# Block inverse of a delta-rule scan: subtractions on GpSimd, products on VectorE

## The chip, the cores and the metric

The kernel runs on one core of one Trainium2 chip. The engines are TensorE (PE in the profile, with PEld for its weight loads), VectorE (DVE), ScalarE (ACT), GpSimd (POOL) and SyncE (SP), which issues most of the DMAs. Every engine works through its own queue of instructions in order and waits at semaphores for the others. The metric is the device time of one execution in microseconds (us).

## The reference

One layer of a backbone over 128 prompt tokens and 2048 sample tokens: a modulated RMSNorm, one wide input projection, three mixers side by side, a gated merge and an output projection. The mixer that matters here is a gated delta rule, computed in chunks; each chunk solves a unit lower triangular system:

```python
m = eye + bc[..., :, None] * jnp.einsum('bnhik,bnhjk->bnhij', kc, kc) * dec_strict
rhs = jnp.concatenate([vc * bc[..., None], kc * (bc * jnp.exp(gam))[..., None]], axis=-1)
sol = lax.linalg.triangular_solve(m, rhs, left_side=True, lower=True, unit_diagonal=True)
...
def step(s, inp):
    u0_, w_, qk_, qg_, kd_, gl_ = inp
    u = u0_ - jnp.einsum('bhck,bhkv->bhcv', w_, s)
    o = jnp.einsum('bhck,bhkv->bhcv', qg_, s) + jnp.einsum('bhij,bhjv->bhiv', qk_, u)
    s = gl_[..., None, None] * s + jnp.einsum('bhck,bhcv->bhkv', kd_, u)
```

The other two mixers are a spatial gate over chunks of 128 tokens (whose norms are called `vss` and whose products `st` below) and a Fourier transform over grid and channels (tiles `xc`, `Y`, `X`, `yT`).

## The kernel before

All GEMMs are written as three float16 products (high by high, high by low, low by high), 512 token columns at a time. They fill TensorE's queue through the whole kernel. The delta mixer runs beside them as a Python generator, `delta()`, that is advanced a step at a time by a pacer: each stretch of GEMM work that is written down lets the generator write down some more of its own instructions. The tile framework then orders each engine's instructions by priority and by its own estimate of when each can run, so a change of engine moves neighbours too.

`delta()` goes through 17 blocks of 128 tokens, in five groups (the prompt block alone, then four groups of four). For each block `prep` normalises keys and queries (row sums on ScalarE, then `ss`, a power of -0.5 on GpSimd), turns tiles on TensorE (`tok`, `T`), forms the triangular matrices (`n`) and stores them (`nd`, `kv` and others, through GpSimd's DMA queue among others). While `prep` works on one group, `base_inverse` inverts the diagonal blocks of the group before: 32 by 32 unit triangular blocks, two directions, one block on each partition. Tile X (in `XB`, first half) holds the blocks, `tmp` (second half of `XB`) the products, E the growing inverse.

The inverse is 31 rounds, from k = 31 down to 1. Round k multiplies k entries of one column of X with 32 - k entries of row k of E, and subtracts these k x (32 - k) products from the rows of E above it. So round k needs E as round k + 1 left it, and `tmp` is written anew in each round. After the rounds four pairs of instructions on ScalarE and VectorE split E into high and low float16 halves, written over `XB`, and DMAs store them (`ei`).

The inverse of the last group, `base_inverse(4)`, is written after all of `prep`. Behind it the pool that holds `XB` and E is closed and another is opened in its place. That one holds the tiles of the scan: `R`, `T`, `Q`, `N`, `ES`, which GpSimd sets to zero, before SyncE loads `ES` and GpSimd copies parts of it into `T` and `R`. The scan's first matmul (`b<-ES,N`) follows. The scan itself needs the inverses in order of the groups.

Around the last inverse the Fourier mixer runs: TensorE makes `X` from PSUM through ScalarE and VectorE, GpSimd copies a mirrored half (`X<-X`), and when a group of channels is done GpSimd forms the gated products `st<-sg,yT` and stores them (`br<-st`).

Four engines are called through a thin recording object, `_InTurn`. It can force the instructions written in certain places to keep their order. Because every call goes through one line of it, nearly all instructions of before bear the line L180 in the profile; tiles tell them apart.

Of the kernel before, what the change touches and what calls it, by code (L numbers as in the profile page):

```python
# [15 lines left out]
ALU = mybir.AluOpType  # L16
# [152 lines left out]
class _InTurn:  # L169


    def __init__(self, tc, engine):
        self.tc, self.engine, self.kept, self.last, self.newest = tc, engine, False, None, None

    def __getattr__(self, name):
        f = getattr(self.engine, name)

        def call(*args, **kw):
            with self.tc.issue_after(self.last.ins) if self.kept and self.last is not None else ExitStack():
                self.newest = f(*args, **kw)  # L180
            if self.kept:
                self.last = self.newest
            return self.newest

        return call

    def queued(self):

        return self.tc.issue_after(self.newest.ins)


@with_exitstack
def hybrid_flow_kernel(ctx: ExitStack, tc: tile.TileContext, x_prompt, x_sample, state_delta, c, c_ctx, w_ada,
# [4 lines left out]
    G, V, A, PE = [_InTurn(tc, e_) for e_ in (nc.gpsimd, nc.vector, nc.scalar, nc.tensor)]  # L198
# [9 lines left out]
    def sb(pl, shape, tag, dt=F32, bufs=None):  # L208
        kw = {} if bufs is None else {"bufs": bufs}
        return pl.tile(list(shape), dt, tag=tag, name=nm(tag), **kw)  # L210
# [31 lines left out]
    newest, gated_, queued = [None], [None], [False]  # L242
# [847 lines left out]
    def base_inverse(g):  # L1090
        nt = len(GROUPS[g])
        nb = 16 * nt
        XB = sb(dq, [P, 2048], "XB")
        X, tmp = XB[:, 0:1024], XB[:, 1024:2048]
        E = sb(dq, [P, 1024], "E")
        if nt < 4:
            V.memset(X, 0.0)
            V.memset(tmp, 0.0)
        b3 = lambda t_: t_.rearrange("p (j i) -> p j i", j=32)
        for d in range(2):  # L1100
            SY.dma_start((X if d == 0 else tmp)[64 * d:64 * d + nb, :], ndD[g][d].rearrange("t h (b j) i -> (t h b) (j i)", b=4))
        for _ in range(8):
            yield 0
        with V.queued():
            V.tensor_copy(b3(X[64:P, :]), tmp[64:P, :].rearrange("p (i j) -> p j i", j=32))
        G.memset(E, 0.0)
        G.memset(E[:, 0:1024:33], 1.0)
        X3, E3 = b3(X), b3(E)
        for k in range(31, 0, -1):
            n_ = 32 - k  # L1110
            t3 = tmp[:, 0:k * n_].rearrange("p (j i) -> p j i", j=k)
            V.tensor_tensor(t3, X3[:, 0:k, k:k + 1].to_broadcast([P, k, n_]), E3[:, k:k + 1, k:32].to_broadcast([P, k, n_]), ALU.mult)
            V.tensor_tensor(E3[:, 0:k, k:32], E3[:, 0:k, k:32], t3, ALU.subtract)
            if k % 2 == 0:
                yield 1
        both = XB.bitcast(F16).rearrange("p (j l w c) -> p j l w c", j=32, l=2, w=2)
        for j0 in (0, 16):
            js = slice(j0, j0 + 16)
            for w, src in ((0, E3), (1, E.rearrange("p (i j) -> p j i", j=32))):
                A.activation(both[:, js, 0, w, :], src[:, js], AF.Copy, scale=FS)  # L1120
                V.scalar_tensor_tensor(both[:, js, 1, w, :], src[:, js], FS, both[:, js, 0, w, :], ALU.mult, ALU.subtract)
                yield 1
            out = [(eD[g][d][js].rearrange("j t (y x) -> (t y) j x", x=128),
                    both[64 * d:64 * d + nb, js].rearrange("p j l w c -> p j (l w c)")) for d in range(2)]
            if g < 4:
                extra.extend(out)
            else:
                SY.dma_start(*out[0])
                A.dma_start(*out[1])
# [277 lines left out]
    def delta():  # L1407
# [5 lines left out]
        for i_, (g, ci, t) in enumerate(seq):  # L1413
            if ci == 0 and g:
                for r_ in base:
                    if r_:
                        yield 1
                base = base_inverse(g - 1)
            for n_, _ in enumerate(prep(g, ci, t, seq[i_ + 1][2] if i_ < 16 else None, held)):
                yield 1  # L1420
                if next(base, 0):
                    yield 1
# [6 lines left out]
        for _ in base_inverse(4):  # L1429
            yield 1  # L1430
# [750 lines left out]
```

## Time and profile before

| what | us |
|---|---|
| three runs | 2149.31, 2153.33, 2158.91 (median 2153.33) |
| the profiled execution, its own time | 2152.75 |
| its span | 2150.9 |
| TensorE busy | 2080.9 |
| VectorE busy | 1363.5 |
| ScalarE busy | 1061.5 |
| GpSimd busy | 751.8 |

The span is what the profiler saw of the profiled execution; 1.85 us lie around it. The mean granted TensorE clock was 0.994. Busy times are sums over the span; the inverses lie between 480 and 876 us, and the scan begins at about 893 us. A row of an engine's timeline reads: start, duration, engine, line, operation, what is written from what, sizes, count, and in brackets the idle time before it and what ended that. The end of a matmul is modelled, so matmuls that follow each other overlap in the rows; their spacing is the start of one to the start of the next.

### The profile page before, as it was taken

What the parts mean: (1) busy time and instruction counts of PE and PEld (TensorE: products, weight loads), DVE (VectorE), ACT (ScalarE), POOL (GpSimd) and SP (SyncE); (2) the same over time, 40 slices, a digit from 0 to 9 for tenths busy, and PEclk for the clock granted to TensorE, in tenths of its full rate; (3) what the DMA queues carried; (4) which work ended last, traced back from release to release, by engine and by line L of the source; (5) the groups of instructions that cost most, each with busy time, mean ns of one, the idle gap of its engine ahead of it and who ended that gap; (6) DMA issues with size and microseconds to landing.
All of it is one profiled execution on the core that took longest, in us unless ns stands there. A gap on an engine that the chain in (4) does not pass through costs nothing.

```text
span 2150.9 us, 42623 instructions
## 1 busy us (share of the span) xinstructions
PE 2080.9 (97%) x16133; PEld 1194.8 (56%) x16133; DVE 1363.5 (63%) x3100; ACT 1061.5 (49%) x2457; POOL 751.8 (35%) x934
## 2 busy tenths in 40 slices
PE   7999999999999999889899999999999999999997
PEld 4454444455555677777555556555655444444443
DVE  6656854389878798566655555766665554666245
ACT  5554744476555664445544445755554353443112
POOL 0321332223333422442322233345443234343464
PEclk9999999999999999999999999999999999999999
DMA  9525732277876743444645555866664645456862
GB/s 353 219 77 191 264 113 92 72 227 224 255 218 223 239 153 98 124 128 136 222 161 167 169 160 188 254 217 207 208 200 137 210 169 175 167 196 234 342 220 89
DMA packets 222910, 403.25 MB, mean 187 GB/s; under 512 B 39720, under 2 KB 109632, under 8 KB 219888
## 3 DMA queue, kind: packets, MB, share of 16 engines
q1 hardware_dynamic: 167664, 290.84, 42.1%
q0 software_dynamic: 15216, 65.89, 8.1%
q10 hardware_dynamic: 39824, 43.79, 6.1%
q8 instruction: 127, 2.08, 0.4%
q14 instruction: 79, 0.65, 0.1%
HBM read 258.19 MB, written 142.24 MB: 186 GB/s over the span
## 4 chain that ended last, share of the span: by engine, by line
PE 70%; DVE 14%; DMA 6%; issue 4%; ACT 3%; POOL 2%; SPq 1%; ACTq 0%; DVEq 0%; POOLq 0%
PE b L180 70%; DVE n L180 2%; DVE XB L180 2%; DVE E L180 1%; DVE sg L180 1%; DMA st<-br 1%; DMA tw<-tw 1%; DMA ab<-in_w_adb_dram 1%; DVE big L180 1%; DVE S L180 1%; DMA ES<-ei 1%; ACT xh L180 0%; DVE X L180 0%; DVE xl L180 0%; DVE xh L180 0%
## 5 line engine op out<-in xcount | busy, mean ns | idle before, releaser
L180 PE MATMUL b<-xh,whi 128*128 128x512 f16 (+1 forms) x1920 | 651.1, 348 | 3.5 <-DVE sg L180 3.5
L180 PE MATMUL b<-xl,whi 128*128 128x512 f16 (+1 forms) x1920 | 651.6, 348 | 0.0
L180 PE MATMUL b<-xh,wlo 128*128 128x512 f16 (+1 forms) x1920 | 650.4, 348 | 0.0
L180 PEld LDWEIGHTS <-whi 128*128 128x128 f16 x3888 | 355.4, 98 | 324.3 <-issue 9.1
L180 PEld LDWEIGHTS <-wlo 128*128 128x128 f16 x1944 | 190.6, 98 | 175.6 <-issue 2.0
L180 PE MATMUL b<-big,bhi 128*128 128x512 f16 (+1 forms) x960 | 251.5, 347 | 2.3 <-ACT big L180 2.0
L180 ACT ACTIVATE sg<-b,winv 128x512 f32<-128x512 f32 (+1 forms) x180 | 110.8, 618 | 160.5 <-PE b L180 155.2
L180 PE MATMUL b<-big,blo 128*128 128x512 f16 (+1 forms) x480 | 163.0, 347 | 0.0
L180 POOL TENSOR_TENSOR mrow<-mrow,sg 128x512 f32<-128x512 f32 (+1 forms) x80 | 92.9, 1163 | 146.4 <-DVE sg L180 113.3
L180 PEld LDWEIGHTS <-xh 128*128 128x128 f16 x1496 | 117.1, 98 | 30.9 <-issue 3.8
L180 POOL TENSOR_TENSOR cy<-cy,raw 128x545 f32<-128x545 f32 (+1 forms) x48 | 65.8, 1396 | 184.3 <-ACT raw L180 184.3
L180 PEld LDWEIGHTS <-bhi 128*128 128x128 f16 x960 | 86.9, 98 | 75.1 <-issue 1.2
L180 PEld LDWEIGHTS <-xl 128*128 128x128 f16 x1068 | 98.1, 98 | 44.9 <-DMA tw<-tw 1.8
L180 PE MATMUL b<-whi,xh 128*128 128x128 f16 x544 | 92.8, 219 | 1.4 <-DVE sg L180 1.4
L180 PE MATMUL b<-whi,xl 128*128 128x128 f16 x544 | 92.8, 219 | 0.0
L180 PE MATMUL b<-wlo,xh 128*128 128x128 f16 x544 | 92.8, 219 | 0.0
L180 DVE SCALAR_TENSOR_TENSOR wlo<-wst,wsc,whi 128x1024 f16<-128x1024 f32 x52 | 68.1, 1311 | 35.0 <-ACT whi L180 34.9
L180 POOL COPY T<-ES 32x256 f16<-32x256 f16 x68 | 29.6, 436 | 159.7 <-DMA ES<-ei 148.3
L180 ACT ACTIVATE whi<-wst,wsc 128x1024 f16<-128x1024 f32 x52 | 59.4, 1143 | 47.8 <-DVE wsc L180 45.1
L180 POOL TENSOR_TENSOR skn<-skn,ed 128x512 f32<-128x512 f32 x34 | 38.0, 1118 | 124.5 <-DMA skn<-kv 119.9
L180 ACT ACTIVATE wlo<-wst 128x1024 f16<-128x1024 f32 x52 | 55.0, 1058 | 47.5 <-DMA wst<-in_w_blk_dram 44.7
L180 DVE SCALAR_TENSOR_TENSOR sg<-b,binv,sg 128x512 f32<-128x512 f32 (+1 forms) x80 | 53.3, 667 | 39.6 <-PE b L180 38.0
(460 smaller groups left out, 4244.4 us busy)
## 6 DMA issues: line engine op xcount, KB each, us to landing
wst<-in_w_blk_dram SPq DMA_DIRECT2D x58, 512.0 KB, 4.5
pa<-pa POOLq DMA_DIRECT2D x16, 896.0 KB, 4.5
qkv<-cy POOLq DMA_DIRECT2D x12, 1089.0 KB, 5.3
st<-br SPq DMA_DIRECT2D x48, 256.0 KB, 3.2
mrow<-mrg SPq DMA_DIRECT2D x16, 576.0 KB, 4.1
pa<-pa SPq DMA_DIRECT2D x5, 1792.0 KB, 11.1
dc<-dec SPq DMA_DIRECT2D x17, 512.0 KB, 6.0
kq<-qkv SPq DMA_DIRECT2D x34, 256.0 KB, 5.0
```

What stands on the lines that cost most here:

```text
L180: self.newest = f(*args, **kw)
```

## The change

In each round of the block inverse the subtraction is issued on GpSimd (`G`); the product stays on VectorE (`V`). All 31 rounds of all five inverses are affected: 155 instructions go from one queue to the other. The recording object is rewritten too: it passes calls through untouched where no order is kept, and looks up the newest instruction of its engine when asked, in place of remembering it. With the subtraction left on VectorE this second part gives the same order on all five engines; it changes the line numbers that the instructions bear.

```diff
     def __getattr__(self, name):
         f = getattr(self.engine, name)
+        if not self.kept:
+            return f
...
     def queued(self):
-        return self.tc.issue_after(self.newest.ins)
+        e = self.engine.engine
+        newest = next((i for i in reversed(self.tc.nc.cur_bb.bb.instructions) if i.engine == e), None)
+        return ExitStack() if newest is None else self.tc.issue_after(newest)
...
             V.tensor_tensor(t3, X3[:, 0:k, k:k + 1].to_broadcast([P, k, n_]), E3[:, k:k + 1, k:32].to_broadcast([P, k, n_]), ALU.mult)
-            V.tensor_tensor(E3[:, 0:k, k:32], E3[:, 0:k, k:32], t3, ALU.subtract)
+            G.tensor_tensor(E3[:, 0:k, k:32], E3[:, 0:k, k:32], t3, ALU.subtract)
```

The orders of all engines are the same up to the first inverse and again from some way into the scan. Between them three places show what moved. The first is GpSimd's queue at the start of the second inverse, while `prep` works on the third group. Before:

```order
L180 DMA nd_3923<-nd_5836 128x4x32
L180 DMA kv_3818<-tok_5924 128x1024
L180 TENSOR_TENSOR ss_752_5925<-ss_752_5925,mhalf_91 128x4
L180 TENSOR_SCALAR rq_1282<-ss_752_5925 128x4
L180 TENSOR_TENSOR st_6072<-sg_6069,vrow_5622 128x512
L180 DMA br_3916<-st_6072 128x512
```

After:

```order
L1074 DMA nd_3923<-nd_5836 128x4x32
L1045 DMA kv_3818<-tok_5924 128x1024
L1115 TENSOR_TENSOR E_5753<-E_5753,XB_5752 128x31
L1465 TENSOR_TENSOR st_6072<-sg_6069,vrow_5622 128x512
L1115 TENSOR_TENSOR E_5753<-E_5753,XB_5752 128x30x2
L1024 TENSOR_TENSOR ss_752_5925<-ss_752_5925,mhalf_91 128x4
L1467 DMA br_3916<-st_6072 128x512
L1115 TENSOR_TENSOR E_5753<-E_5753,XB_5752 128x29x3
L1038 TENSOR_SCALAR rq_1282<-ss_752_5925 128x4
L1115 TENSOR_TENSOR E_5753<-E_5753,XB_5752 128x28x4
```

A norm (`ss`), a gate product (`st`) and a store now stand between subtractions, and each is behind one that waits for VectorE.

The second place is GpSimd's queue at the end of the last inverse and the start of the scan. Before:

```order
L180 COPY X_1092_8298<-X_1092_8298 128x4x63 x2
L180 TENSOR_TENSOR st_10527<-sg_10172,yT_9570 128x512
L180 TENSOR_TENSOR st_10531<-sg_10231,yT_9570 128x512
L180 TENSOR_TENSOR st_10535<-sg_10329,yT_9570 128x512
L180 DMA br_3917<-st_10527 128x512
L180 MEMSET R_1272_10504 128x1024
```

After:

```order
L1115 TENSOR_TENSOR E_9690<-E_9690,XB_9689 128x4x28
L1465 TENSOR_TENSOR st_10527<-sg_10172,yT_9570 128x512
L1465 TENSOR_TENSOR st_10531<-sg_10231,yT_9570 128x512
L1465 TENSOR_TENSOR st_10535<-sg_10329,yT_9570 128x512
L1115 TENSOR_TENSOR E_9690<-E_9690,XB_9689 128x3x29
L1467 DMA br_3917<-st_10527 128x512
L1467 DMA br_3917<-st_10531 128x512
L1467 DMA br_3917<-st_10535 128x512
L1115 TENSOR_TENSOR E_9690<-E_9690,XB_9689 128x2x30
L1465 TENSOR_TENSOR st_10567<-sg_10564,yT_9570 128x512
L1465 TENSOR_TENSOR st_10599<-sg_10596,yT_9570 128x128
L1115 TENSOR_TENSOR E_9690<-E_9690,XB_9689 128x31
```

Five gate products and three stores stand inside the last three rounds; before, the products came after the inverse and three of them ahead of the scan's memsets.

The third place is TensorE's queue at the scan's first matmul (the one that reads `ES`). Before:

```order
L180 MATMUL b_10854<-wlo_9675,xh_94 128x128
L180 LDWEIGHTS xl_95
L180 MATMUL b_10854<-whi_9674,xl_95 128x128
L180 LDWEIGHTS N_1275_10510
L180 MATMUL b_10784<-ES_10512,N_1275_10510 128x32
```

After:

```order
L250 MATMUL b_11224<-xl_95,whi_10061 128x512
L250 LDWEIGHTS wlo_10062
L250 MATMUL b_11224<-xh_94,wlo_10062 128x512
L250 LDWEIGHTS N_1275_10510
L250 MATMUL b_10784<-ES_10512,N_1275_10510 128x32
```

It stands 24 matmuls of 512 columns and 192 of 128 columns later than before, in another unit of the Fourier mixer. These matmuls are then missing in the stretch that follows: up to the first use of the scan's state (`b<-S,sk`) there are 180 matmuls of 128 columns fewer than before.

More of the change, by code (lines that the diff above doesn't have):

```diff
@@ L172, in __init__ @@
     def __init__(self, tc, engine):
-        self.tc, self.engine, self.kept, self.last, self.newest = tc, engine, False, None, None
+        self.tc, self.engine, self.kept, self.last = tc, engine, False, None
     def __getattr__(self, name):
         f = getattr(self.engine, name)
+        if not self.kept:
+            return f
         def call(*args, **kw):
[L179 to L183, printed above, removed]
+            with self.tc.issue_after(self.last.ins) if self.last is not None else ExitStack():
+                self.last = f(*args, **kw)
+            return self.last
         return call
     def queued(self):
-        return self.tc.issue_after(self.newest.ins)
+        e = self.engine.engine
+        newest = next((i for i in reversed(self.tc.nc.cur_bb.bb.instructions) if i.engine == e), None)
+        return ExitStack() if newest is None else self.tc.issue_after(newest)
 @with_exitstack
```

## The prediction

> **What bounds the kernel now.** I read the page's first lines, then what TensorE waited for between 470 and 900 us (the stretch that holds the five block inverses), then the busy time of each engine in the stretches of the inverses, and last the instructions themselves.
>
> ```profile
> span 2150.9 us, 42623 instructions
> PE 2080.9 (97%) x16133; PEld 1194.8 (56%) x16133; DVE 1363.5 (63%) x3100; ACT 1061.5 (49%) x2457; POOL 751.8 (35%) x934
> ```
>
> TensorE (PE) has work in 97% of the span, and only 70 us are idle. What a change on VectorE (DVE) or GpSimd (POOL) can win is a part of these 70 us; what it can lose has no such limit.
>
> ```profile
> 480.00:557.00 77.00, 76.85 (x546) 45.15 (x545) 71.67 (x202) 43.93 (x136) 24.93 (x32) 1.00 0.79 244
> 557.00:640.00 83.00, 78.58 (x508) 44.55 (x507) 71.59 (x169) 49.93 (x150) 31.53 (x39) 0.98 0.71 223
> 640.00:740.00 100.00, 98.47 (x599) 53.32 (x598) 79.12 (x190) 58.82 (x180) 41.46 (x50) 1.00 0.73 230
> 740.00:822.00 82.00, 79.91 (x1091) 67.72 (x1090) 75.17 (x202) 54.14 (x158) 28.38 (x40) 1.00 0.51 167
> 822.00:892.00 70.00, 62.93 (x822) 49.74 (x819) 48.92 (x130) 28.60 (x59) 21.68 (x31) 1.00 0.40 108
> ```
>
> After the length of the stretch the columns are the busy time of PE, weight loads, DVE, ACT and POOL. The first four rows hold one inverse each, the fifth the last inverse. VectorE is busy 86 to 93% in three of the first four, GpSimd about a third; yet PE is idle for 8.2 us in these four and for 7.1 us in the fifth.
>
> ```profile
> PE b L180 <- DVE sg L180: 3.7, 4, 1.5
> PE b L180 <- POOL T L180: 2.4, 1, 2.4
> PE b L180 <- DVE xc L180: 2.0, 3, 1.4
> PE b L180 <- ACT yT L180: 1.6, 1, 1.6
> PE b L180 <- DVE T L180: 1.2, 3, 0.8
> PE b L180 <- DVE X L180: 1.1, 3, 0.5
> ```
>
> These are the six longest of PE's named waits there (total, times, longest). Those on VectorE sum to 8.0 us: this is nearly all that a relieved VectorE can give back.
>
> **The change, part by part.** *Removed from VectorE: 155 subtractions.*
>
> ```profile
> L180 DVE TENSOR_TENSOR E<-E,XB x155: 190/365/1273, 486.9 to 870.0; 128x31 f32<-128x31 f32 x10, 128x60 f32<-128x60 f32 x10, 128x87 f32<-128x87 f32 x10, 128x112 f32<-128x112 f32 x10
> L180 DVE SCALAR_TENSOR_TENSOR XB<-E,XB x20: 679/862/1067, 556.3 to 873.5; 128x512 f16<-128x512 f32 x20
> 830.00:876.00 46.00, 24.68 (x66) 3.15 (x4) 0.00 (x0) 1.00 0.17 43
> sum 385.00, DVE 126.17 ACT 13.99 POOL 3.29; mean DVE 25.23 ACT 2.80 POOL 0.66
> ```
>
> The last two rows are for tile E alone. Of 126.2 us, 20 splits at a mean of 0.87 us are 17; half of the remaining 109 us are the subtractions: 55 us, 11 us per inverse. Of the last inverse's 24.7 us the four splits take 3.4, and half the rest, 10.7 us, is its 31 products.
>
> *Added to GpSimd: the same 155.*
>
> ```profile
> L180 POOL TENSOR_TENSOR st<-sg,yT 128x512 f32<-128x512 f32 x16 | 20.0, 1270 | 21.9 <-DVE wscb L180 10.3 <-DVE E L180 5.0 <-DVE yT L180 3.9
> L180 POOL TENSOR_TENSOR st<-sg,yT 128x128 f32<-128x128 f32 x4 | 1.8, 456 | 1.4 <-DMA br<-st 1.3
> L180 POOL TENSOR_TENSOR ss<-ss,mhalf 128x4 f32<-128x4 f32 x34 | 36.8, 1084 | 46.4 <-DVE ss L180 41.9 <-DVE vss L180 3.8 <-DVE bss L180 0.2
> L180 POOL DMA_DIRECT2D br<-st x40 | 23.4, 586 | 4.1 <-POOL st L180 3.3 <-POOL E L180 0.4 <-DMA kT<-T 0.3
> L180 POOL COPY X<-X 128x252 f16<-128x252 f16 x32 | 15.1, 480 | 58.9 <-ACT X L180 43.5 <-DVE X L180 15.1
> br<-st POOLq DMA_DIRECT2D x32, 256.0 KB, 2.9
> ```
>
> From 128 elements (456 ns) to 512 (1270 ns) an f32 operation of two inputs grows by 2.12 ns an element, over a fixed 185 ns. Round k has k(32-k) elements, 5456 in 31 rounds: 31 x 0.185 + 5456 x 0.00212 = 17.3 us per inverse, 87 us in all, against 55 us taken off VectorE.
>
> *Added: two hand-overs a round.* The product must now be seen by GpSimd and the difference by VectorE.
>
> ```profile
> 876.54 1.04 DVE L180 TENSOR_TENSOR yT<-b,us 128x256 f32<-128x256 f32 x2
> 877.67 3.73 POOL L180 TENSOR_TENSOR st<-sg,yT 128x512 f32<-128x512 f32 x3 [10.34 <-DVE wscb L180]
> 2124.45 1.07 POOL L180 TENSOR_TENSOR hss<-hss,mhalf 128x1 f32<-128x1 f32 x1
> 2125.55 1.28 DVE L180 SCALAR_TENSOR_TENSOR xh<-xh,hss,fg 128x1024 f32<-128x1024 f32 x1 [0.44 <-POOL hss L180]
> ```
>
> VectorE ends at 877.58 and GpSimd starts at 877.67 (0.09 us); GpSimd ends at 2125.52 and VectorE starts at 2125.55 (0.03). 31 x 0.12 = 3.7 us an inverse. The bare chain of one inverse is then 10.7 + 17.3 + 3.7 = 31.7 us.
>
> *First four inverses.* Each has 82 us or so and its result is wanted only later, so a chain of 32 us plus what it queues behind fits; the PE order hardly moves there. What counts is the queue: the order puts norms (1.08 us each), DMA issues and gate products between the subtractions on GpSimd, each now behind a subtraction that waits for a product. PE then waits for the turned tokens that need those norms. Against that, VectorE has 11 us less per stretch. Bounds: half of the 8.0 us back (-4), or 13 blocks of tokens each 0.9 us late, one full norm less what covers it (+12). I take +3, nearer to the gain, since GpSimd stays under 60% busy ((31.5 + 17.3)/83).
>
> *Last inverse.* It has no such slack: the scan's tiles reuse its memory, so the memsets wait for its end.
>
> ```profile
> 834.61 1.04 DVE L180 COPY XB<-XB 64x1024 f32<-64x1024 f32 x1 [3.98 <-DMA XB<-nd]
> 835.74 0.21 DVE L180 TENSOR_TENSOR XB<-XB,E 128x31 f32<-128x31 f32 x1
> 870.01 0.19 DVE L180 TENSOR_TENSOR E<-E,XB 128x31 f32<-128x31 f32 x1
> 881.93 0.97 POOL L180 MEMSET R<- 128x1024 f16 x1
> 891.72 1.54 POOL L180 COPY T<-ES 32x256 f16<-32x256 f16 x2 [0.25 <-DMA ES<-ei]
> 893.38 0.45 PE L180 MATMUL b<-ES,N 128*128 128x32 f16 x8 [2.44 <-POOL T L180]
> ```
>
> Now the 31 rounds take 34.5 us (835.74 to 870.20), the memset starts 11.7 us later, and PE, which arrived at 890.94, waits 2.4 us for the tile T. After the change: 31.7 us bare chain; eight X copies in GpSimd's order (3.8 us, half of it behind products: 2); three gate products of 1.27, three DMA issues of 0.59, and two more products (1.27 and 0.46) between the last rounds (7.3), one of which waits some 2 us for a store that takes 2.9; the 43 other VectorE instructions, mostly in the shadow of subtractions (4, estimate). Together 47 us, and the start is 2 us later, since two evictions stand ahead of the copy now: the end moves by 47 + 2 - 34.5 = +14. The three gate products (3.7 us) stood between the end and the memset before and no longer do; stores still have to land, so I count 2 us back: the scan is ready +12 us later.
>
> *Cover.* In the new order 24 matmuls of 512 columns and 192 of 128 more stand ahead of the scan's first matmul.
>
> ```profile
> 837.80 0.22 PE L180 MATMUL b<-wlo,xh 128*128 128x128 f16 x1
> 838.70 0.22 PE L180 MATMUL b<-whi,xl 128*128 128x128 f16 x1
> 839.08 0.38 PE L180 MATMUL b<-xl,whi 128*128 128x512 f16 x1
> 840.59 0.38 PE L180 MATMUL b<-xh,wlo 128*128 128x512 f16 x1
> ```
>
> First and last of 17 and of 8 rows: one every 56 and 216 ns. 24 x 0.216 + 192 x 0.056 = 15.9 us of cover for a delay of 12: the 2.4 us wait goes. But this work then lacks further on: the order catches up within the first scan step, which took from 893.4 to the state's first use at 923 with about 12 us of GEMM that only filled. With 10 us less filling the step nears its bare latency; I take 5 us of new waits (0 to 14, the second if nothing in the step shrinks). Beside it the Fourier stage waits for X copies that now stand behind subtractions: +2 (-3, its VectorE waits gone, to +6, eight copies each a round of 0.8 us late).
>
> **Sum.** +3 + 2 - 2.4 + 5 = +7.6 us. Nothing behind it can win this back, since the order is then the same and PE is the bound. The profiled execution took 2152.75 us, 0.6 below the median of 2153.33: 2160.4, rounded to 2160.
>
> **A rule to weigh.** The row first: GpSimd and VectorE already hold each other up.
>
> ```profile
> 667.30 1.26 POOL L180 TENSOR_TENSOR st<-sg,vrow 128x512 f32<-128x512 f32 x1 [0.99 <-DVE sg L180]
> 667.46 1.28 DVE L180 TENSOR_TENSOR XB<-XB,E 128x156 f32<-128x156 f32 x1
> 839.53 0.32 DVE L180 TENSOR_TENSOR XB<-XB,E 128x156 f32<-128x156 f32 x1
> ```
>
> A product of 156 elements takes 0.32 us alone and 1.28 us when a GpSimd product is running; it ends 0.18 us after that one. So each subtraction can hold the next VectorE instruction that reads two tiles of SBUF, and the other way round. The Trainium skill, "SBUF — State Buffer", section "Who interferes with whom", says that a VectorE instruction with two SBUF inputs contends with a GpSimd instruction that reads SBUF, under an exclusive lock; this row agrees with it. By the Trainium skill's rule the sum would be that of rival three, 2165, and by the row's single case 2160: a product cannot collide with the subtraction that waits for it, only the other instructions can.
>
> **Rivals.** *One, the cover runs out.* A round costs more than 1.0 us: from 16 + 2.4 - 12 = 6 us more, 0.2 us a round, every microsecond of the last chain is PE's. At 1.4 us a round it is 12 us later, 6 of them uncovered, and the prep stretches go to their +12: 2153 + 7.6 + 6 + 9 = 2175. For it: strided operands of 1 to 31 elements a row, which no GpSimd row here shows. Against it: every GpSimd row quoted here follows its element count, and 11.6 of the 17.3 us come from that count.
> *Two, VectorE's relief wins.* If prep's norms are not late, PE gets back 4 to 8 of the 8.0 us, and the scan's start costs nothing: 2153 - 2.4 - 4 to -8 = 2143 to 2147, just faster. For it: VectorE at 93% in the first stretch. Against: PE idles 0.15 us in that very stretch. It decides if a norm waits under 0.3 us more than now.
> *Three, the lock.* If every one of 155 subtractions holds a VectorE instruction for half its length (87/155/2 = 0.28 us), 43 of the 55 us come back as blocking, and the prep term goes from +3 to the middle of its bounds' upper half, +8: 2165. For it: the 1.28 us row. Against it: most other VectorE instructions in these stretches read PSUM and one tile.
>
> **Chances.** Forecast 0.52 (2150 to 2172; 0.36 of it within 0.5%), rival one 0.20, two 0.20 (0.06 of it faster by over 0.5%), three 0.08 (half and half). 0.5% is 10.8 us, about what this kernel's runs, 2149 to 2159, can tell. Faster 0.06, same 0.36 + 0.14 + 0.04 = 0.54, slower 0.16 + 0.20 + 0.04 = 0.40. The range: below, rival two's upper part, 2146; above, rival one with 6 us more, 2181.
>
> **What would show it.** Right: in the after profile DVE busy falls by about 55 us and POOL's rises by about 87; tile E's GpSimd rows have medians near 0.55 us; the last inverse takes 44 to 50 us from first product to last subtraction; PE's wait for T at the scan's start is under 3 us; PE idle grows by some 8 us, all between 480 and 950 us. Wrong: subtractions near 1 us, PE waiting for tok or T in each block of tokens, or a wait of over 8 us at the scan's first matmul (rival one); PE idle below 10 us up to 892 us (rival two).

## The result and the profile after

The changed kernel takes 2148.53 us (median of 9 runs, 2145.90 to 2153.26), the kernel before 2155.11 us in the same session (9 runs, 2149.31 to 2158.91). The ratio is 0.9972, 95% interval 0.9962 to 0.9983: 6 us, or 0.28%, faster. The forecast was 2160 us, 7.6 us slower. A second measurement of the same order of instructions (e_sub_only below) gives 0.9967 (0.9956 to 0.9978).

First the page's head, after. The profiled execution took 2150.54 us.

```profile
span 2148.7 us, 42636 instructions
PE 2085.8 (97%) x16133; PEld 1198.8 (56%) x16133; DVE 1328.0 (62%) x2945; ACT 1062.1 (49%) x2457; POOL 840.1 (39%) x1089
```

GpSimd gained 88 us, as forecast (87). VectorE lost only 35.5 us, not 55. The two profiled spans differ by 2.2 us, the medians by 6.6: a single execution lies up to some 6 us from its median (before's profiled one was 2.4 us below, this one 2.0 above). The traces therefore tell where time moved, and the ratios how much.

The busy time by stretch, after; the columns are those of the prediction's table (length, then PE, weight loads, VectorE, ScalarE, GpSimd, granted clock). The last stretch holds the scan's start; its row of before follows in a fence of its own.

```profile
480.00:557.00 77.00, 75.52 (x519) 43.08 (x517) 67.00 (x174) 45.65 (x139) 41.90 (x63) 1.00 0.75 237
557.00:640.00 83.00, 80.62 (x545) 45.83 (x544) 62.91 (x141) 50.73 (x157) 51.65 (x72) 1.00 0.75 241
640.00:740.00 100.00, 100.00 (x656) 56.24 (x655) 72.45 (x164) 58.36 (x175) 57.63 (x81) 1.00 0.72 228
740.00:822.00 82.00, 78.31 (x1039) 65.80 (x1037) 65.82 (x165) 55.82 (x163) 46.86 (x74) 0.98 0.50 164
822.00:892.00 70.00, 69.23 (x953) 57.10 (x951) 42.35 (x99) 27.60 (x57) 33.18 (x56) 1.00 0.33 86
892.00:960.00 68.00, 59.39 (x747) 46.85 (x745) 37.96 (x93) 31.92 (x78) 33.68 (x53) 0.90 0.50 145
```

```profile
892.00:960.00 68.00, 60.96 (x829) 47.79 (x830) 38.20 (x92) 31.43 (x81) 28.65 (x50) 0.97 0.42 123
```

PE's idle time is the length less its busy time. In the four stretches of the first inverses it is 7.6 us after 8.2: waits moved from one place to another there, but their sum hardly changed. In the fifth, the last inverse beside the Fourier mixer, it is 0.8 us after 7.1; 1.1 us of the 7.1 is the beginning of the wait for `T` at the scan's start (890.94 to 892), so 6.0 belong to the stretch itself. From 892 to 960 us it is 8.6 after 7.0 (8.1 with that 1.1), and the clock there is 0.90 after 0.97.

The named waits of PE from 470 to 900 us, after (total, times, longest):

```profile
PE b L1049 <- DVE tok L1033: 2.7, 3, 1.5
PE b L250 <- DVE sg L1455: 1.8, 1, 1.8
PE b L250 <- DVE T L1051: 1.4, 3, 1.0
PE b L250 <- ACT T L1050: 1.2, 2, 0.9
PE b L250 <- ACT yT L1661: 0.9, 2, 0.5
```

The waits for `xc` and `X` (3.1 us together in the prediction's list) are gone or, for `X`, down to 0.2 us; those for `sg` halved; the wait for the turned tokens `tok` grew from 0.2 us, and one for `T` from ScalarE is new. One row of before, the second longest, is not in the prediction's list; the profile names no releaser for it:

```profile
PE b L180 <- issue: 3.1, 2, 2.4
```

It is gone too.

Tile E's two groups that matter (duration in ns, least, median and most; first and last start):

```profile
L1115 POOL TENSOR_TENSOR E<-E,XB x155: 240/606/1601, 485.8 to 878.1; 128x31 f32<-128x31 f32 x10, 128x60 f32<-128x60 f32 x10, 128x87 f32<-128x87 f32 x10, 128x112 f32<-128x112 f32 x10
L1123 DVE SCALAR_TENSOR_TENSOR XB<-E,XB x20: 670/1031/1479, 552.9 to 882.0; 128x512 f16<-128x512 f32 x20
```

A subtraction on GpSimd has a median of 0.61 us, and the 155 of them sum to 94.0 us (mean 607 ns). The splits on VectorE rose from a median of 0.86 us to 1.03. The last inverse and the scan's start, from the timeline:

```profile
835.32 0.21 DVE L1114 TENSOR_TENSOR XB<-XB,E 128x31 f32<-128x31 f32 x1
878.10 0.25 POOL L1115 TENSOR_TENSOR E<-E,XB 128x31 f32<-128x31 f32 x1
899.76 0.83 POOL L1188 COPY T<-ES 32x256 f16<-32x256 f16 x2 [3.17 <-DMA ES<-ei]
900.65 0.18 PE L250 MATMUL b<-ES,N 128*128 128x32 f16 x1 [0.55 <-POOL T L1188]
910.07 0.47 PE L250 MATMUL b<-ES,N 128*128 128x32 f16 x8 [3.66 <-DMA ES<-ei]
937.12 0.45 PE L250 MATMUL b<-ES,N 128*128 128x32 f16 x8 [2.20 <-DMA ES<-ei]
```

The last inverse takes 43.0 us (835.32 to 878.35) after 34.5, and the scan's first matmul stands 7.3 us later. PE waits 0.55 us for it after 2.44, but then 3.66 and 2.20 us for later loads of `ES`, where the filling work is missing that now lies ahead of the scan.

### The profile page after: what moved, and what is told of

Same layout as the page of the kernel before. It is cut to its first block, busy times and chain, and to the rows that moved or that the text cites. A ratio compares the mean times of both kernels' runs of the same rounds, so it can differ in the third digit from the quotient of the medians.

```text
span 2148.7 us, 42636 instructions
## 1 busy us (share of the span) xinstructions
PE 2085.8 (97%) x16133; PEld 1198.8 (56%) x16133; DVE 1328.0 (62%) x2945; ACT 1062.1 (49%) x2457; POOL 840.1 (39%) x1089
## 4 chain that ended last, share of the span: by engine, by line
PE 50%; DVE 8%; DMA 7%; POOL 3%; ACT 3%; issue 3%; SPq 0%; ACTq 0%; DVEq 0%; POOLq 0%
PE b L250 50%; DMA st<-br 2%; DMA pa<-pa 1%; DMA ES<-ei 1%; POOL E L1115 1%; DVE XB L1114 1%; DVE big L1692 1%; ACT nd L1066 1%; POOL ss L1024 1%; POOL st L1465 0%; ACT big L1691 0%; DVE n L1083 0%; DMA wst<-in_w_blk_dram 0%; DVE sg L476 0%; DVE n L1064 0%
## 5 line engine op out<-in xcount | busy, mean ns | idle before, releaser
L1115 POOL TENSOR_TENSOR E<-E,XB 128x31 f32<-128x31 f32 (+15 forms) x155 | 94.0, 607 | 84.6 <-DVE XB L1114 67.8
L1725 ACT ACTIVATE sg<-b,winv 128x512 f32<-128x512 f32 (+1 forms) x120 | 74.0, 616 | 94.0 <-PE b L250 93.4
L315 ACT ACTIVATE wlo<-wst 128x1024 f16<-128x1024 f32 x52 | 54.9, 1056 | 58.2 <-DMA wst<-in_w_blk_dram 54.8
L1114 DVE TENSOR_TENSOR XB<-XB,E 128x31 f32<-128x31 f32 (+15 forms) x155 | 55.3, 357 | 41.7 <-POOL E L1115 41.1
```

The source lines that it names most:

```text
L315: w.squared = A.activation(w.lo, st, AF.Square, accum_out=ss)
L1115: G.tensor_tensor(E3[:, 0:k, k:32], E3[:, 0:k, k:32], t3, ALU.subtract)
L1725: gated_[0] = A.activation(sg, ps, AF.Sigmoid, scale=gw.inv)
```

## The experiments

The first theory, A, is the prediction's rival two: VectorE's relief takes PE's waits away. Theory B is that the new order wins, which puts 15.9 us of GEMM work ahead of the scan's first matmul. Three more (S, P and Q) were formed when these two failed for the first four inverses, and stand in the expectations. Each kernel is the changed one with the edit shown, unless it says otherwise; ratios are to the kernel before, measured on the same chip beside it, with their 95% intervals. "PE idle" is taken from the busy time of the same stretches in each profile.

### What the recording object does, and where the gain lies

Control, all subtractions back on VectorE:

```diff
-            G.tensor_tensor(E3[:, 0:k, k:32], ...)
+            V.tensor_tensor(E3[:, 0:k, k:32], ...)
```

> Control: the rewritten recording object alone, all subtractions left on VectorE; the order of all engines is that of before. Both theories: the time of before, ratio 1.000 within 0.002. A ratio as low as the changed kernel's 0.997 would mean that the gain is not the subtractions' at all.

Measured 1.0002 (0.9988 to 1.0015). Its profile shows much the same waits of PE as before; at the scan it is 3.1 us for `N` in place of 2.4 for `T`. The other half of the control moves the subtraction in the old kernel:

```diff
-            V.tensor_tensor(E3[:, 0:k, k:32], ...)
+            G.tensor_tensor(E3[:, 0:k, k:32], ...)
```

> The subtraction moved in the old kernel, without the rewritten recording object: the order of all engines is that of the changed kernel. All theories: the changed kernel's ratio, 0.9972 within 0.0015.

Measured 0.9967 (0.9956 to 0.9978); its profile has the waits of the changed kernel, the two for `ES` too (3.56 and 2.06 us). So the time is the subtraction's alone, and the waits are a property of the order, not chance of one execution. Next, the two halves of the change:

```diff
+            (G if g < 4 else V).tensor_tensor(...)      # e_first_four
+            (G if g == 4 else V).tensor_tensor(...)     # e_last_only
```

> Subtractions on GpSimd in the first four inverses only, the last one all on VectorE. Theory A (VectorE's relief: what PE waited for VectorE goes, wherever an inverse runs): the profile after stood 4 us ahead at 790 us, so -3 to -4 us, ratio 0.998 to 0.9985. Theory B (the order: what won is the GEMM work that the scheduler put ahead of the scan's first matmul, which only the last inverse moves): 0, ratio 1.000 within 0.001. My forecast's own term for this part was +3 us (ratio 1.0014).

> Subtractions on GpSimd in the last inverse only. Theory A: PE's waits from 822 to 892 us (7 us) nearly go, and some 4 to 5 us come back as waits at the scan's start: -2 to -3 us, ratio 0.9985 to 0.999. Theory B: the whole gain, -6 us, ratio 0.997. My forecast's terms for this part were +2 - 2.4 + 5 = +4.6 us (ratio 1.002).

Measured 0.9985 (0.9973 to 0.9997), some 3.2 us, and 0.9990 (0.9976 to 1.0005), some 2.2 us. They add up to the whole within their intervals, though the second interval holds 1.000, so that this half alone isn't shown to be faster. Theory B, which gave everything (0.997) to the last inverse, falls. The last inverse alone, 822 to 892 and 892 to 960 us, and the scan's first matmul:

```profile
822.00:892.00 70.00, 66.12 (x888) 53.45 (x886) 41.97 (x98) 27.46 (x59) 33.24 (x55) 1.00 0.31 77
892.00:960.00 68.00, 59.06 (x796) 46.68 (x794) 40.07 (x95) 33.79 (x83) 33.97 (x57) 0.95 0.51 157
```

```profile
900.77 0.39 PE L250 MATMUL b<-ES,N 128*128 128x32 f16 x5 [7.54 <-DMA N<-n]
```

PE gets 2.1 us back beside the Fourier mixer (idle 3.9 us after 6.0). Not all of this need be the moved work: e_first_four, whose last inverse stays on VectorE, is idle 4.1 us there too (5.2 less the 1.1 that belong to its wait at the scan), though at a clock of 0.98. PE pays at the scan, where it now waits 7.5 us in place of 2.4: in this order only 3.6 us more of GEMM work stands ahead of the scan (worked out from the order as the prediction did), against 15.9 in the changed kernel.

### Is it VectorE's load?

e_no_sub takes the subtractions out and sets E to zero:

```diff
-        G.memset(E[:, 0:1024:33], 1.0)
+        G.memset(E[:, 0:1024:33], 0.0)
...
-            G.tensor_tensor(E3[:, 0:k, k:32], ...)
```

> The subtractions are left out altogether and E is zero, so the inverse is not computed; VectorE still loses its 55 us and GpSimd gets nothing. It prices the relief alone. Theory A: all VectorE waits of PE in 480 to 900 us may go (8 us), and the last inverse ends at some 855 us, 15 us earlier than before, so that PE never waits for T (2.4 us more): -8 to -11 us, ratio 0.995 to 0.996; GpSimd's price in the real change is then the difference, 2 to 5 us. Theory B: the order is another one, so there is no reason for a gain beyond the 2.4 us: ratio 0.999.

Measured 0.9973 (0.9961 to 0.9986): no more than the real change. The fourth and fifth of its stretches:

```profile
740.00:822.00 82.00, 77.08 (x1044) 64.88 (x1042) 66.22 (x173) 55.64 (x162) 30.77 (x43) 1.00 0.60 183
822.00:892.00 70.00, 67.03 (x879) 54.13 (x877) 38.76 (x97) 29.26 (x62) 24.98 (x39) 0.95 0.34 96
```

Where the first four inverses run, PE is idle for 11.4 us (8.2 before), though VectorE has lost 35 us there: the last `sq` starts at 798.6 us, after 798.1 before. The gain lies in the last stretch and the scan's start. Beside the last inverse PE is idle 3.0 us after 6.0, but the clock of 0.95 there takes some 3 us back; what stays is the scan's start, where the first matmul comes at 886.59 us, 6.8 us early, and waits for nothing. So in this order relief alone does not pay in the first four, and in the last it pays by the earlier end. VectorE's total is 1319.0 us: taking the subtractions away saves 44.5 us of busy time, 9 us more than moving them to GpSimd does.

Half of the rounds, and twice the work on each engine:

```diff
+            (G if k % 2 else V).tensor_tensor(...)      # e_even_k
```

> Only the odd rounds (16 of 31) subtract on GpSimd, the even ones on VectorE, in all five inverses. Half of VectorE's relief, half of GpSimd's price; but in this order no more GEMM work stands ahead of the scan's first matmul than in before. Theory A (relief): about half the gain, -3 us, ratio 0.9985. Theory B (the GEMM work put ahead of the scan): 0, ratio 1.000.

Measured 1.0022 (1.0010 to 1.0035): slower, and both theories were wrong. VectorE has 14 us less in the first four stretches, PE idles 8.8 us there (8.2 before), and the scan's first matmul waits 3.6 us at 897.5. Why half of the rounds cost time stays open.

```diff
+            V.tensor_tensor(t3, X3[...], E3[...], ALU.mult)     # twice
+            V.tensor_tensor(E3[:, 0:k, k:32], ...)              # e_double_v
```

> Subtractions on VectorE as in before, and each product written twice (the second time the same values), so VectorE carries some 55 us more than before, 11 us per inverse; the order puts 21 us more of GEMM work ahead of the scan's first matmul than before does. Theory A: PE's waits on VectorE (8 us in before) grow by about as much as the change made them shrink: +4 to +8 us, ratio 1.002 to 1.004. Theory B: with the cover of the changed kernel and more it should be faster too, ratio 0.997 to 0.999.

Measured 1.0113 (1.0098 to 1.0128), some 24 us slower, three times the most that theory A gave. PE's idle time over the first four goes to 15.7 us, and the last inverse starts at 862.7 us, 27 us late; the scan's first matmul then waits 13.95 us. So more work on VectorE does cost PE time in these stretches, where less work (e_no_sub) gave none back.

```diff
             G.tensor_tensor(E3[:, 0:k, k:32], ...)
+            G.tensor_tensor(t3, E3[:, 0:k, k:32], t3, ALU.subtract)   # e_double_g
```

> As the changed kernel, and behind each subtraction a second GpSimd instruction of the same shape that writes the used-up products' place (its values are not used); the next product must wait for it. GpSimd carries another 90 us, a round takes some 0.6 us more, the last inverse some 18 us more, with only 5 us more cover. Theory A with a GpSimd that is free: the first four inverses keep their gain of 3 us, the last one costs 13 us uncovered and the clock's dip behind it: +8 to +12 us, ratio 1.004 to 1.006. If GpSimd's queue had a price in the first four inverses as my forecast had it (+3 us and more with twice the load), ratio 1.008.

Measured 1.0343 (1.0329 to 1.0357), 74 us slower: far off.

```profile
914.05 0.27 POOL L1115 TENSOR_TENSOR E<-E,XB 128x31 f32<-128x31 f32 x1 [11.20 <-DVE XB L1114]
984.89 0.47 PE L250 MATMUL b<-ES,N 128*128 128x32 f16 x8 [68.85 <-POOL T L1189]
```

The first four no longer fit into their 82 us each (the first takes 94 us from its first product to its last subtraction), so the fourth ends at 897 us and the last begins only at 913.8, with all of it uncovered. It is a loss of rival one's kind, though by another way: the first four run late and push the last one back. In the changed kernel the first four take 58 to 67 us (45 to 71 before). How long they may become before this sets in was not measured.

The rounds spaced without moving work, in the first four inverses:

```diff
+            V.tensor_tensor(E3[:, 0:k, k:32], ...)
+            if g < 4:
+                G.tensor_copy(E3[:, k - 1:k, 31:32], E3[:, k - 1:k, 31:32])
```

> All subtractions on VectorE, as in before; in the first four inverses each is followed by a copy of one element of the row of E that the next product reads, onto itself, on GpSimd. VectorE keeps its whole load; only its rounds no longer run back to back, since each product waits for GpSimd. Theory S (spacing: what PE waits for are evictions stuck behind a burst of rounds in VectorE's queue, and the hand-over breaks the burst up): the gain of the first four inverses comes without moving any work, ratio 0.998 to 0.999. Theory A (relief: VectorE's load must fall): no gain, or a loss by the longer rounds, ratio 1.000 to 1.003.

Measured 1.0079 (1.0067 to 1.0092): theory S falls as far as this run can test it. Each round pays two hand-overs and VectorE's own subtraction, the first inverse takes 87 us, PE idles 16.5 us over the first four; spacing without longer rounds was not tried.

### The first four inverses in parts

```diff
+            (G if g < 4 and 8 < k < 24 else V).tensor_tensor(...)      # e_four_big
+            (G if g < 4 and not 8 < k < 24 else V).tensor_tensor(...)  # e_four_small
+            (G if g < 4 and k % 2 == 0 else V).tensor_tensor(...)      # e_four_evens
```

> First four inverses only: the 15 large rounds (k = 9 to 23, 65% of the elements) subtract on GpSimd, the 16 small ones and the last inverse on VectorE. Theory A (the gain follows the work that leaves VectorE): some 60% of the 3 us of all 31 rounds, ratio 0.999; more than the two runs beside it. Theory P (places: the gain is what a few evictions of VectorE and the transposes behind them happen to wait in the one order or the other, without regard to the size moved): anything from 0.997 to 1.004, and no ranking by size.

> The complement: the 16 small rounds (k = 1 to 8 and 24 to 31, 35% of the elements) of the first four inverses subtract on GpSimd. Theory A: some 40% of the gain, ratio 0.9995, less than with the large rounds. Theory P: 0.997 to 1.004, no ranking.

> First four inverses only, every second round (k even, 15 rounds, 50% of the elements) on GpSimd. Theory A: half the gain, ratio 0.9993, between the two others. Theory P: 0.997 to 1.004, no ranking; as the odd rounds of all five inverses were 4.7 us slower, a loss is as likely as a gain.

Measured 1.0050 (1.0035 to 1.0064), 1.0001 (0.9991 to 1.0011) and 1.0029 (1.0018 to 1.0040). The more elements are moved, the slower, until all are moved and it is faster: no price per moved microsecond fits this. Theory A falls for the first four inverses; theory P, which claimed no more than that places decide, is not refuted, and explains nothing by itself. VectorE is busy 279 to 284 us in the four stretches (298 before, 267 with all rounds moved), and PE idles 15.6, 10.2 and 14.9 us (8.2 and 7.2). The worst single wait, in e_four_big, with ScalarE's queue (its DMA issues and the eviction behind them) ahead of it:

```profile
639.16 1.50 ACTq L1003 DMA_DIRECT2D ei<-XB  x1
640.70 2.86 ACTq L998 DMA_DIRECT2D qk<-n  x1
643.60 0.69 ACT L1453 ACTIVATE sg<-b,winv 128x512 f32<-128x512 f32 x1 [5.20 <-issue]
645.13 0.58 PE L250 MATMUL b<-xh,whi 128*128 128x512 f16 x1 [5.05 <-DVE sg L1455]
```

ScalarE evicts `sg` only when it has issued five DMAs in a row, from 636.1 to 643.6 us; VectorE waits for ScalarE and PE for VectorE. The kernel before has the same run at 631.5 (6.8 us) and 724.8 (6.2 us); where all rounds move, the second and third inverse end 15 and 8 us later, and the runs there are 2.4 and 3.8 us. To test whether that is the gain, the stores `ei` were given to SyncE's queue:

```diff
             if extra:
-                A.dma_start(*extra.pop(0))
+                SY.dma_start(*extra.pop(0))
```

> All subtractions on VectorE; the stores of an ended inverse (ei) of the first four inverses are issued by SyncE instead of ScalarE. Theory Q (ScalarE's queue: the first-four gain of the change is that the run of DMA issues in front of the eviction sg falls apart): PE's waits for sg at 640 and 692 us shrink, and some 2 to 3 us are gained without moving a subtraction, ratio 0.9985 to 0.999. Theory P (places, by luck of the order): any ratio from 0.997 to 1.004.

> Subtractions of the first four inverses on GpSimd, and their stores ei issued by SyncE. Theory Q: the two remedies are for the same wait, so hardly more than the subtractions alone (0.9985): 0.998 to 0.9988. If they are for different waits they add up: 0.997.

Measured 0.9994 (0.9983 to 1.0004) with all subtractions on VectorE and 0.9966 (0.9954 to 0.9977) with those of the first four on GpSimd. The wait for `sg` at 640 us is gone without moving a subtraction, but no gain can be told from the noise. That run alone leaves theory Q open, since Q's 0.9985 to 0.999 lies inside its interval. The second run decides: Q gave 0.998 to 0.9988, and 0.9966 is what two separate gains would give. Theory Q falls as the explanation of the gain. What is left in the first of the two:

```profile
586.63 0.63 PE L1016 MATMUL b<-cst,qr 128*128 128x128 f32 x4 [2.66 <-issue]
692.68 0.38 PE L250 MATMUL b<-xh,whi 128*128 128x512 f16 x1 [1.09 <-DVE sg L1455]
```

Both waits are in the kernel before too (2.37 and 1.51 us), and in the changed kernel neither is; but right behind the place of the first, at 587 us, PE waits 1.76 us for `sg` there.

### The last inverse's end

```diff
+            (V if g == 4 and k < 8 else G).tensor_tensor(...)     # e_mix8
+            (V if g == 4 and k < 16 else G).tensor_tensor(...)    # e_mix16
+            (V if g == 4 and k > 23 else G).tensor_tensor(...)    # e_mixr8
```

> As the changed kernel, but the last seven rounds of the last inverse subtract on VectorE, so that gate products and stores in GpSimd's queue no longer stand between them: the last inverse should end some 6 us earlier; 8.6 us less of GEMM work stands ahead of the scan. Theory A: PE's waits at the scan's start (3.66 and 2.2 us, with the clock's dips) shrink: 2 to 4 us faster than the changed kernel, ratio to before 0.9955. Theory B: less cover, part of the gain is lost, ratio 0.9985.

> As the changed kernel, but the last fifteen rounds of the last inverse subtract on VectorE (seven in the run before). The last inverse ends another 3 us or so earlier, and 4.5 us less of GEMM work stands ahead of the scan than there. If the scan's start were still what the last inverse's end decides: ratio 0.994 to 0.9955. If VectorE's relief in the Fourier stretch (822 to 892 us) is worth as much: the same as there or worse, 0.996 to 0.998 (with no round of it on GpSimd, 0.9985).

> The mirror of e_mix8: in the last inverse the first eight rounds (k = 24 to 31) subtract on VectorE, the other 23 on GpSimd, its last ones among them, between which the gate products and stores stand. If e_mix8 gained by the end of the last inverse no longer waiting for GpSimd's queue: no gain here over the changed kernel, ratio 0.997. If it gained because fewer rounds of the last inverse hand over: the same as e_mix8, 0.9957.

Measured 0.9957 (0.9944 to 0.9969), 0.9968 (0.9956 to 0.9981) and 0.9968 (0.9956 to 0.9980). The copy that makes `T` ready in e_mix8, and the scan's first matmul:

```profile
895.73 0.84 POOL L1188 COPY T<-ES 32x256 f16<-32x256 f16 x2 [2.39 <-DMA ES<-ei]
896.71 0.19 PE L250 MATMUL b<-ES,N 128*128 128x32 f16 x1 [4.24 <-POOL T L1188]
```

It is 4 us earlier than in the changed kernel (899.76), and the waits of 3.66 and 2.20 us inside the scan's first step are not there; the first matmul waits 4.24 us instead of 0.55. The mirror, e_mixr8, keeps them (3.60 and 1.88) and the changed kernel's time. So it seems to be the end of the last inverse, or the filling work that stays in the scan's first step, that pays; these runs don't separate the two, and the intervals of e_mix8 and e_mixr8 overlap. With fifteen rounds on VectorE (e_mix16) `T` is ready another 3.3 us earlier, but PE arrives earlier still and the first matmul waits 7.1 us. Last, e_mix8 with `ei` on SyncE:

> The fastest kernel so far (all subtractions on GpSimd but the last seven rounds of the last inverse) with the stores ei on SyncE. Theory Q: as without, ratio 0.9957 within 0.0015. If the two add up: 0.994.

Measured 0.9955 (0.9942 to 0.9968), median 2144.11 us against 2155.41 beside it. With e_mix8 (2145.65 against 2153.53) this is the fastest of all; the intervals overlap that of the changed kernel. Here the stores on SyncE add nothing to e_mix8, as theory Q said, while they seemed to add to e_first_four.

## Why the prediction was wrong

*"Nearly all that a relieved VectorE can give back" (8.0 us):* too low. The list left out the wait put down to `issue` (3.1 us), most of which stands behind an eviction of VectorE, as shown below, and the clock that such a wait costs.

*VectorE's removed load (55 us):* the size was right, 155 rows with 54.8 us in all (mean 354 ns), but busy time counts overlapping rows once, and a row often starts before the one ahead has ended (`sg` at 691.94 us in a fence below, while the product ahead of it ends at 692.02). So only 44.5 us go where nothing is put on GpSimd, and 35.5 in the changed kernel. Of the 9 us between the two, at most that much is rival three's blocking (it gave 43): the splits' median of 1.03 us is 0.95 in e_no_sub, with no subtraction on GpSimd, and 0.86 before, so about half of their rise came without it.

*GpSimd's added load (87 us) and the rate of 2.12 ns an element:* near enough. The page gained 88 us, the rows sum to 94.0, and the median is 0.61 us against 0.55. The bare chain of 31.7 us stands alone in no run.

*First four inverses, +3 (-4 to +12):* this step failed. Measured -3.2 us (ratio 0.9985), inside its bounds, at their other end. The mechanism it named was there: the turned tokens did wait more for norms in GpSimd's queue. The waiters of tile `ss`, before and after (us, times):

```profile
  DVE tok L180: 2.8, 6
  PE b L180: 1.1, 2
```

```profile
  DVE tok L1033: 4.3, 8
  PE b L1049: 2.7, 3
```

It cost most at the last blocks of tokens. There PE, from 790 to 800 and from 800 to 810 us, before and after:

```profile
790.00:800.00 10.00, 9.13 (x82) 6.22 (x80) 9.68 (x27) 5.58 (x26) 2.47 (x4) 1.00 0.21 77
800.00:810.00 10.00, 9.20 (x93) 6.17 (x91) 10.00 (x34) 5.83 (x16) 4.58 (x8) 1.00 0.50 173
```

```profile
790.00:800.00 10.00, 6.59 (x80) 5.50 (x79) 8.02 (x25) 5.72 (x26) 7.08 (x13) 1.00 0.20 76
800.00:810.00 10.00, 9.95 (x84) 7.09 (x84) 9.56 (x26) 5.04 (x13) 4.08 (x7) 0.83 0.50 172
```

After the change PE waits 0.48 us for `yT`, 1.11 for `tok`, 0.87 and 1.00 for `T`, and the clock falls to 0.83: 5.2 us lost, against 1.7 before. Up to this place the changed kernel had gained 4.2 us (the last `sq` starts at 793.9 us after 798.1). Behind it, at 810 us, PE is 0.5 us ahead of the kernel before, counted by the starts of its matmuls at equal work done; e_first_four is 0.5 us ahead there too, and so is the control with no subtraction moved. So within the first four stretches loss and gain about cancel, and most of the 3.2 us shows only further on.

The forecast, by its queue argument, took the cost for larger than what a relieved VectorE gives back. Against it stand waits that went. The clearest one is at 692 us in the kernel before, VectorE's queue and PE:

```profile
691.16 0.42 DVE L180 TENSOR_TENSOR E<-E,XB 128x247 f32<-128x247 f32 x1
691.61 0.41 DVE L180 TENSOR_TENSOR XB<-XB,E 128x240 f32<-128x240 f32 x1
691.94 0.74 DVE L180 SCALAR_TENSOR_TENSOR sg<-b,winv,sg 128x512 f32<-128x512 f32 x1
692.74 0.38 PE L180 MATMUL b<-xh,whi 128*128 128x512 f16 x1 [1.51 <-DVE sg L180]
```

The eviction `sg` stands behind rounds of the inverse that run back to back. After the change no two rounds can run back to back on VectorE, since each product waits for GpSimd. The other is at 585 us, where before an eviction of `n` stands behind a subtraction and `q`, and PE waits 2.37 us; that this eviction frees PE's bank is read from the times, since the profile names no releaser:

```profile
583.37 0.38 DVE L180 TENSOR_TENSOR E<-E,XB 128x220 f32<-128x220 f32 x1
583.66 0.74 DVE L180 SCALAR_TENSOR_TENSOR q<-qr,qsc,q 128x512 f16<-128x512 f32 x1
584.33 0.69 DVE L180 TENSOR_TENSOR n<-b,dc 128x512 f32<-128x512 f32 x1
585.12 1.09 PE L180 MATMUL b<-cst,qr 128*128 128x128 f32 x4 [2.37 <-issue]
```

After the change that eviction is done at 582.9 us. These readings describe the two orders; they are no rule, and e_spaced_four, where no two rounds run back to back either, was slower. Seven other ways to load VectorE and GpSimd in the first four stretches (e_no_sub, e_even_k, e_double_v, e_spaced_four and the three parts) are 0.5 to 9.5 us late at the last `sq`. What makes the full move better than each part of it stays open: the scheduler writes another order for each, and no run here holds the order fixed while the load changes.

*Last inverse, 34.5 to 47 us, scan ready +12:* right in kind, too large: 43.0 us, and the scan's first matmul +7.3. The gate products and stores did stand between the last rounds, from 869.95 to 878.1 us.

*Fourier stage, +2 (-3 to +6):* this step failed, and it is the larger error. PE's idle time there went from 6.0 to 0.8 us, -5.2, beyond the lower bound. The waits for `xc` and `sg` went from this stage, those for `X` and `yT` shrank. Where the order puts little more GEMM work ahead of the scan, 2 to 3 us of the idle time go (e_last_only 3.9 us idle, e_no_sub 3.0); with more such work the rest goes too (e_mix8 1.8, the changed kernel 0.8). The prediction counted that work as cover for the scan's start only. But e_mix16, with 2.8 us more of it, is idle only 1.5 us there outside its wait at the scan. So whether this work or VectorE's lighter queue fills the stage, these orders don't separate.

*Wait for T, -2.4, and new waits in the scan's first step, +5:* -1.9 (2.44 to 0.55 us) and +2.4 (the other idle time, 5.7 to 8.1 us), near enough. What the sum put at nothing, without a reason, is the clock: 4.0 us at the scan's start. The granted clock stands at the third number from the end of these rows, two microseconds each; before, behind the wait at 585:

```profile
584.00:586.00 2.00, 0.89 (x5) 0.85 (x6) 2.00 (x5) 1.38 (x6) 0.00 (x0) 0.77 0.27 64
586.00:588.00 2.00, 2.00 (x20) 2.00 (x19) 2.00 (x5) 2.00 (x9) 1.33 (x1) 0.50 0.90 234
588.00:590.00 2.00, 2.00 (x15) 1.21 (x13) 1.93 (x6) 2.00 (x12) 1.68 (x3) 0.88 1.03 345
```

And after the change, behind the waits at 910 and 937:

```profile
910.00:912.00 2.00, 1.93 (x27) 1.93 (x28) 0.42 (x1) 0.51 (x2) 1.40 (x4) 0.55 0.06 17
918.00:920.00 2.00, 2.00 (x27) 2.00 (x26) 1.19 (x4) 1.24 (x4) 1.39 (x4) 0.50 0.27 96
938.00:940.00 2.00, 2.00 (x22) 2.00 (x21) 1.32 (x5) 1.76 (x7) 1.58 (x4) 0.50 0.14 35
```

The wait of 2.37 us cost more than half as much again in the clock: 0.2, 1.0 and 0.2 us of busy time lost in the three rows, some 1.4. The scan's start lost 5.5 us that way after the change and 1.5 before (busy time times one less the clock, summed over such rows from 892 to 960). So a wait of PE has to be priced with what it does to the clock.

Put together, the profiles show some -0.5 us for the first four inverses, -5.2 for the Fourier stage and +4.5 for the scan's start, about -1 us, where the two spans differ by 2.2 and the medians by 6.6. A good part of the measured gain thus lies in no term that these two profiled executions show.

*"Nothing behind it can win this back", and rival two:* nothing did win it back; it was won ahead of it. Rival two's sign is there: PE idle 8.3 us from 480 to 892 us, under the 10 that it gave; and as a change from 2153 its 2143 to 2147 is 6 to 10 us, which holds the measured 6.6. That is in part luck. Its condition, that the norms are not late, was not met (PE waited 2.7 us for `tok` after 0.2), the waits that went were mostly those of the Fourier stage, and the scan's start, which it took as free, did cost. The evidence that was weighed against it, that PE idled 0.15 us in the stretch where VectorE was at 93%, was a reading of one stretch, while the waits that went lay in the others. Rival one was weighed rightly: the cover held, with a wait of 0.55 us at the scan's first matmul.

## What to carry to other kernels

A price per moved microsecond tells little where an engine has slack on average and its queue is in order: list the single waits of the bounding engine in the stretch, and ask for each what stands ahead of the releaser in its queue, and whether the change takes that away. Look at each stretch that the moved work overlaps, not only at those where its own result is waited for; here the largest term was the stage that ran beside it. After such a move, try the last rounds of a chain on the old engine: seven of 31 back in place gave the best times here, by a margin that the intervals don't yet separate.

## What the runs showed of the hardware

Waits of PE of 2.37 us at 585 us (before) and 2.20 us at 937 us (after) were followed by rows of the clock at 0.50, while 2.44 us at 893 us before and 1.76 us at 587 us after were not. Four shorter waits close together, 0.48 to 1.11 us each from 794 to 800 us after the change, were followed by a row at 0.50 as well. The Trainium skill, "TensorE: Matmul & The Clock Gate", section "Why this matters for your kernels", asks for no idle gaps over some 3 us; these two profiles show drops behind single gaps of 2.20 and 2.37 us, and not behind every gap of that size.

An issue of one of the stores `qk` and `n` by ScalarE takes 0.33 us when it stands alone, and up to 2.86 us (`qk` in e_four_big) in the run with the stores `ei` of an inverse. With `ei` on SyncE (e_ei_sp_before), `qk` and `n` are issued in 0.33 to 0.34 us each at that place, and ScalarE is free for its evictions.
